# Where the multiplier table of the S5 scan is written: behind the initial states, at the end of a step

## The chip, the cores and the metric

The kernel runs on one core of a Trainium2 chip. The metric is the device time of one execution in microseconds (us), lower is better. The engines are named as in the profile: PE is TensorE (matmuls; PEld its weight loads), DVE is VectorE, ACT is ScalarE, POOL is GpSimd, and SP issues most of the DMAs. Each engine works through its own list of instructions in order, and waits on semaphores for the others.

## The reference, cut to what matters

A decoder of two layers works on 512 prompt tokens and on 8 x 4 sample tokens, 544 columns together. Layer 0 mixes tokens by gated linear attention, layer 1 by an S5 layer, and each is followed by an MLP of width 4096. The change lies in the S5 layer, a diagonal complex recurrence over the sequence:

```
u = xn @ w_in
bu = einsum(u, bb)                    # per group of 16 channels, 64 complex states
h[t] = lam * h[t-1] + bu[t]           # lam = mag * (cos + i sin), per state
y = Re(einsum(h, c)) + d_skip * u
z = gelu(y)
out = (z @ w_glu_a) * sigmoid(z @ w_glu_b)
```

All arithmetic is float32 in the result. Matmuls of the large weights are made of three products of high and low parts.

## The kernel before, in words

**Weights.** A large matrix is cut into tiles of 128 columns (1024 x 128). SP loads a tile `raw`; ACT casts it to the high part `wh` (L126, two halves of 128x512); DVE (L131) and POOL (L133) subtract to get the low part `wl`. A planner spreads these halves over the matmul jobs some jobs ahead of their use. One job is 24 matmuls on one tile and one half of the columns; a half is 288 or 256 columns.

**The recurrence.** The 64 groups of states are handled as 16 units. The complex recurrence is turned into a real one: every four tokens are gathered into one column (`n`), the values are rotated by a table of cosines and sines, a real scan with a decay per state runs along the 128 columns of prompt time, and the result is rotated back. The decay per step of four tokens is the column `self.r4`. The scan instruction wants a multiplier for each element, so `radius(u)` writes the table `rr` (128 x 2 x 2 x 128) with two ACT instructions at L1300 that copy a row of ones times `r4`. There is only one `rr`, so the table of unit u+1 may be written only after the scan of unit u has read it.

**Steps.** A software pipeline of steps (`beat(i)`), numbered -2 to 21, carries four units at once. In the order of the code, step i holds:

- `outs(i-3)`: PE multiplies the states by the output tables into `yp` (L1328, L1330); ACT makes the gelu (L1333); SP stores it to scratch `yd` (L1335).
- `states(i)`: PE makes the inputs of unit i, `wp` (L1273).
- `scan(i-2)`: DVE scans (L1308), then `radius(i-1)` on ACT (L1300), then, in some steps, `zl`, the low part of finished blocks of z (L1348), then the rotation back on DVE (L1312, L1313, L1314) and two tiny sums for the final state on POOL (L1317).
- `turned(i-1)`: POOL completes the rotation of unit i-1 (L1293, L1294), which its scan will read.
- `turn(i)`: DVE rotates `wp` of unit i (L1284, L1285, L1286); ACT copies the sample columns of `wp` into `S` (L1289, twice).
- loads by SP for later units: `load_q` (tables `qt` and `m`), `load_w` (`wt`, `ct`), `load_u` (`U`).
- `before(i-1)`: ACT writes the initial states of the samples into `area` (L1320).
- in some steps: ACT casts a finished block of z to `zh` (L1350), SP loads blocks of z (L1339).

`area` is one large buffer that holds the scan's input and output for two units, among other things; so the profile calls many of these tiles `area`.

The steps -2 to 11 are hung behind the jobs of the S5 input projection, one or two to a job:

```
BEATS = {5:(-2,),6:(-1,),7:(),8:(0,1),9:(2,),10:(3,4),11:(5,),12:(6,7),13:(8,),14:(9,10),15:(11,)}
```

So of the steps that scan, 2, 4, 5, 7, 8 and 10 are the last behind their job: the next things on ACT, DVE and POOL are the casts and subtractions of a weight tile (L126, L131, L133), then on DVE the evacuation of the job's PSUM bank (`u_out`, L1249), and only then the next scan. Steps 3, 6 and 9 are followed at once by another step, and so are 11 to 15, which run on after the last job with matmuls of the GLU that follows (`advance`, L237 on `zh`, `zl`) between them on PE.

Nothing is reordered: each engine gets its instructions in the order in which the code issues them.

Of the kernel before, what the change touches and what calls it, by code (L numbers as in the profile page):

```python
# [79 lines left out]
class Builder:  # L80
# [1105 lines left out]
    def s5(self, ctx):  # L1186
# [45 lines left out]
        def load_w(u):  # L1232
            for i in (0, 1):
                nc.sync.dma_start(table(u, i), self.wd[u][:, 512 * i:512 * i + 512])

        def load_q(u):
            if u < 16:
                nc.sync.dma_start(qt[u % NQ], self.qd[u])
                m = p.tile([128, 2, 128], F32, tag="m", name="m", bufs=NQ)
                for q in (0, 1):  # L1240
                    base = self.md[2 * u + q]
                    src = bass.AP(tensor=base.tensor, offset=base.offset, ap=[[256, 32], [32, 4], [1, 128]])
                    nc.sync.dma_start(m[:, q], src)
                st[u]["m"] = m
# [9 lines left out]
        def load_u(u):  # L1254
            if u < 16:
                m, q = divmod(u, 2)
                U = p.tile([128, 2, 136], F32, tag="U", name="U", bufs=6)
                d = self.ud[m]
                src = bass.AP(tensor=d.tensor, offset=d.offset + 272 * q, ap=[[4 * 136, 32], [128 * 136, 4], [1, 272]])
                nc.sync.dma_start(U.rearrange("p q n -> p (q n)"), src)  # L1260
                st[u]["U"] = U

        def cs(u):
            return table(u, 1).rearrange("p (t q n) -> p t q n", t=2, q=2)

        def states(u):

            w, U = table(u, 0), st[u]["U"]
            ps = []
            for r in (0, 1):  # L1270
                g = self.bank("wp")[:, :272].rearrange("p (q n) -> p q n", q=2)
                for q in (0, 1):
                    nc.tensor.matmul(g[:, q], w[:, r * 256 + q * 128:r * 256 + (q + 1) * 128], U[:, q],  # L1273
                                     start=True, stop=True)
                ps.append(g)
            st[u]["ps"] = ps

        def turn(u):

            ps, c = st[u].pop("ps"), cs(u)  # L1280
            tp = [self.p_t.tile([128, 288], F32, tag="sq", name="rot", bufs=5)[:, :256].rearrange("p (q n) -> p q n", q=2)
                  for _ in range(2)]
            re, im = ps[0][:, :, 8:136], ps[1][:, :, 8:136]
            V.tensor_mul(A["g"][u % 2], re[:, None].to_broadcast([128, 2, 2, 128]), c)  # L1284
            V.tensor_mul(tp[1], im, c[:, 1])  # L1285
            V.tensor_mul(tp[0], im, c[:, 0])  # L1286
            st[u]["tp"] = tp
            for r in (0, 1):
                nc.scalar.activation(ws[r][:, 2 * u:2 * u + 2], ps[r][:, :, 0:8], AF.Copy)  # L1289

        def turned(u):
            g, tp = A["g"][u % 2], st[u].pop("tp")
            G.tensor_tensor(g[:, 0], g[:, 0], tp[1], op=OP.add)  # L1293
            G.tensor_tensor(g[:, 1], tp[0], g[:, 1], op=OP.subtract)  # L1294

        def radius(u):

            ones = self.cst[:, C_ONE:C_ONE + 127]
            for q in (0, 1):
                nc.scalar.activation(rr[:, :, q, 1:128], ones[:, None].to_broadcast([128, 2, 127]), AF.Copy,  # L1300
                                     scale=self.r4[:, 2 * u + q:2 * u + q + 1])

        def scan(u, between):

            g, c = A["g"][u % 2], cs(u)
            oc, os = A["c"][u % 2][:, :, :, 9:137], A["s"][u % 2][:, :, :, 9:137]
            flat = lambda v: v.rearrange("p r q n -> p (r q n)")
            V.tensor_tensor_scan(flat(g), flat(rr), flat(g), 0.0, OP.mult, OP.add)  # L1308
            if u < 15:
                radius(u + 1)  # L1310
            between()
            V.tensor_mul(oc, g, c[:, None, 0].to_broadcast([128, 2, 2, 128]))  # L1312
            V.tensor_mul(os[:, 0], g[:, 0], c[:, 1])  # L1313
            V.scalar_tensor_tensor(os[:, 1], g[:, 1], -1.0, c[:, 1], op0=OP.mult, op1=OP.mult)  # L1314
            oc, os = A["c"][u % 2], A["s"][u % 2]
            for r in (0, 1):
                G.tensor_tensor(fs[:, r, 2 * u:2 * u + 2], oc[:, r, :, 136], os[:, 1 - r, :, 136], op=OP.add)  # L1317

        def before(u):
            nc.scalar.activation(A["c"][u % 2][:, :, :, 0:8], h0[:, :, 2 * u:2 * u + 2], AF.Copy)  # L1320

        def outs(u):
            s = st[u]
            q5 = qt[u % NQ]
            oc, os = A["c"][u % 2], A["s"][u % 2]
            ps = self.bank("yp")[:, :272].rearrange("p (q n) -> p q n", q=2)
            for q in (0, 1):
                nc.tensor.matmul(ps[:, q], s["m"][:, q], s["U"][:, q], start=True, stop=False)  # L1328
                for i, (r, h) in enumerate(((0, oc[:, 0]), (1, oc[:, 1]), (1, os[:, 0]), (0, os[:, 1]))):
                    nc.tensor.matmul(ps[:, q], q5[:, r * 256 + q * 128:r * 256 + q * 128 + 128], h[:, q, 0:136],  # L1330
                                     start=False, stop=(i == 3))
            y = A["y"][u % 2]
            nc.scalar.activation(y, ps, AF.Gelu_apprx_tanh)  # L1333
            m, half = divmod(u, 2)
            nc.sync.dma_start(self.yd[m].rearrange("t (e q) n -> (t e) q n", q=4)[:, 2 * half:2 * half + 2], y)  # L1335

        def load_z(m):
            for t in range(4):
                nc.sync.dma_start(A["z"][m % NZ][:, t], self.yd[m][3 - t])  # L1339

        def split_z(m, low):

            z = A["z"][m % NZ]
            if "h" not in Z:
                Z["h"] = self.p_p.tile([128, KD, NT], F32R, tag="Hh", name="zh")
            place = lambda v: v[:, m].rearrange("p (t c) -> p t c", t=4)
            if low:
                V.tensor_sub(place(Z["l"]), z, f32(place(Z["h"])))  # L1348
            else:
                nc.scalar.activation(place(Z["h"]), z, AF.Copy)  # L1350

        def beat(i):

            live = lambda j: 0 <= j < 16
            for m in Z_LOAD.get(i, ()):
                load_z(m)
            if live(i - 3):
                outs(i - 3)
            if live(i):
                states(i)  # L1360
            lo = lambda: [split_z(m, True) for m in Z_LOW.get(i, ())]
            if live(i - 2):
                scan(i - 2, lo)
            else:
                lo()
            if live(i - 1):
                turned(i - 1)
            if live(i):
                turn(i)
            if i >= 3:  # L1370
                load_q(i - 3 + NQ)
            if i in LW:
                load_w(LW[i])
            load_u(i + 2)
            if live(i - 1):
                before(i - 1)
            for m in Z_CAST.get(i, ()):
                split_z(m, False)
            for m in Z_LOAD_LAST.get(i, ()):
                load_z(m)  # L1380
# [10 lines left out]
        for s, beats in BEATS.items():  # L1391
            for i in beats:
                self.after[J + s].append(lambda i=i: beat(i))
# [5 lines left out]
        for i in range(done + 1, last + 1):  # L1399
            beat(i)  # L1400
            if i >= ZB + LAG:
                k = min((i - ZB - LAG) // 2 + 1, KD - 1)
                more = [(2, 0), (3, 0), (2, 1), (3, 1)][:max(0, i - FB + 1)]
                for t, hf in [(0, 0), (1, 0), (0, 1), (1, 1)] + more:
                    self.advance(self.tile0 + t, hf, zh, zl, k, t > 1)
# [206 lines left out]
```

## Time and profile before

| what | value |
|---|---|
| median of 3 runs (lowest, highest) | 1327.24 us (1324.19, 1329.14) |
| the profiled execution: its own time | 1327.25 us |
| the profiled execution: span of the trace | 1325.5 us |
| PE busy in the span | 1284.5 us (97%) |
| DVE busy | 746.7 us (56%) |
| ACT busy | 618.5 us (47%) |
| POOL busy | 445.9 us (34%) |
| first and last write of `rr` (L1300) | 722.4 us, 823.7 us |
| first and last scan (L1308) | 742.3 us, 827.0 us |
| in 738 to 842 us: PE, DVE, ACT, POOL busy | 93.05, 77.44, 39.32, 44.79 us of 104 |

How to read it: outside the S5 steps PE is busy all the time, and over the whole span it is busy 97%. The S5 steps lie between 738 and 842 us; there PE is idle for 11 us. In a timeline row the columns are start (us), duration of the merged pieces (us), engine, line, operation, output<-input, count, and in brackets the idle time of that engine just before the row with the instruction that is taken to have ended it. That name is inferred; where several semaphores were waited for, it need not be the one that decided.

### The profile page before, as it was taken

How to read it: one execution, taken by the hardware profiler on the slowest of the kernel's cores; microseconds unless marked ns; L12 is line 12 of the kernel's file. 1: busy time of each engine (PE TensorE's matmuls, PEld its weight loads, DVE VectorE, ACT ScalarE, POOL GpSimd, SP SyncE). 2: the span in 40 equal slices, each digit the busy share in tenths (PEclk: the TensorE clock that was granted, in tenths of full speed). 3: DMA queues.
4: the chain of work that ended last, by engine and by line, in shares of the span. 5: the costliest groups of instructions: out<-in, count | busy, mean ns of one | idle time of the engine just before them, and what ended most of it. 6: DMA issues, size and time to landing. Idle time of an engine off the chain costs nothing. (4 is left out here: it accounts for less than half of the span.)

```text
span 1325.5 us, 25660 instructions
## 1 busy us (share of the span) xinstructions
PE 1284.5 (97%) x9966; PEld 1260.1 (95%) x9966; DVE 746.7 (56%) x1747; ACT 618.5 (47%) x1394; POOL 445.9 (34%) x603
## 2 busy tenths in 40 slices
PE   7999999999999999999998988999999999999996
PEld 6999999999999999999998988999999999999996
DVE  7866564557436667666458678445721332332345
ACT  7633454566426657556444343446633432431432
POOL 4444244622371111111321443542223343242241
PEclk9999999999999999999999999999999999999998
DMA  5233322474324555545345688345523223232222
GB/s 192 96 132 107 104 69 84 129 183 99 105 81 162 156 165 175 169 139 154 100 119 182 185 249 239 98 138 135 121 65 112 80 80 96 80 96 80 80 65 68
DMA packets 83130, 164.67 MB, mean 124 GB/s; under 512 B 9313, under 2 KB 45409, under 8 KB 81985
## 3 DMA queue, kind: packets, MB, share of 16 engines
q1 hardware_dynamic: 77824, 144.16, 35.0%
q0 software_dynamic: 5184, 18.88, 6.3%
q8 instruction: 78, 1.28, 0.4%
q14 instruction: 44, 0.35, 0.1%
HBM read 137.54 MB, written 25.46 MB: 123 GB/s over the span
## 5 line engine op out<-in xcount | busy, mean ns | idle before, releaser
L133 POOL TENSOR_TENSOR wl<-raw,wh 128x384 fp32r<-128x384 f32 (+3 forms) x315 | 300.3, 964 | 549.0 <-ACT wh L126 544.0
L237 PE MATMUL held<-xh,wh 128*128 128x256 f32 (+1 forms) x1344 | 392.1, 292 | 0.1
L237 PE MATMUL held<-xl,wh 128*128 128x256 f32 (+1 forms) x1344 | 389.5, 290 | 0.0
L237 PE MATMUL held<-xh,wl 128*128 128x256 f32 (+1 forms) x1344 | 387.8, 289 | 0.1
L237 PE MATMUL held<-hh,wh 128*128 128x256 f32 (+1 forms) x1024 | 296.2, 289 | 0.7 <-ACT acc L440 0.7
L237 PE MATMUL held<-hl,wh 128*128 128x256 f32 (+1 forms) x1024 | 296.1, 289 | 0.0
L237 PE MATMUL held<-hh,wl 128*128 128x256 f32 (+1 forms) x1024 | 294.7, 288 | 0.0
L126 ACT ACTIVATE wh<-raw 128x512 fp32r<-128x512 f32 x332 | 198.6, 622 | 125.7 <-PE held L237 79.4
L237 PEld LDWEIGHTS held<-xh,wh 128*128 128x128 f32 x1344 | 254.4, 189 | 2.4 <-issue 1.4
L237 PEld LDWEIGHTS held<-xl,wh 128*128 128x128 f32 x1344 | 254.0, 189 | 0.4
L237 PEld LDWEIGHTS held<-xh,wl 128*128 128x128 f32 x1344 | 253.5, 189 | 0.3 <-DMA wl<-in_w 0.3
L131 DVE TENSOR_TENSOR wl<-raw,wh 128x128 fp32r<-128x128 f32 (+3 forms) x321 | 169.9, 542 | 106.8 <-ACT wh L126 100.4
L237 PEld LDWEIGHTS held<-hh,wh 128*128 128x128 f32 x1024 | 193.2, 189 | 2.6 <-issue 1.2
L237 PEld LDWEIGHTS held<-hl,wh 128*128 128x128 f32 x1024 | 193.0, 188 | 0.1
L237 PEld LDWEIGHTS held<-hh,wl 128*128 128x128 f32 x1024 | 192.6, 188 | 0.0
L432 ACT ACTIVATE r<-r 128x256 f32<-128x256 f32 (+1 forms) x128 | 55.0, 429 | 166.6 <-DVE r L430 166.5
L442 DVE TENSOR_TENSOR acc<-held,acc 128x288 f32<-128x288 f32 (+1 forms) x96 | 42.2, 439 | 120.8 <-PE held L237 120.7
L434 DVE TENSOR_TENSOR hl<-r,hh 128x256 fp32r<-128x256 f32 (+1 forms) x128 | 56.4, 441 | 83.1 <-ACT hh L433 82.6
L430 DVE SCALAR_TENSOR_TENSOR r<-held,rs 128x256 f32<-128x256 f32 (+1 forms) x128 | 56.1, 438 | 76.1 <-PE held L237 75.6
L237 PE MATMUL held<-zl,wh 128*128 128x288 f32 (+1 forms) x240 | 69.0, 288 | 1.4 <-DVE zl L1348 1.2
L237 PE MATMUL held<-zh,wh 128*128 128x288 f32 (+1 forms) x240 | 69.4, 289 | 0.0
L237 PE MATMUL held<-zh,wl 128*128 128x288 f32 (+1 forms) x240 | 68.7, 286 | 0.0
(393 smaller groups left out, 2044.3 us busy)
## 6 DMA issues: line engine op xcount, KB each, us to landing
raw<-in_w SPq DMA_DIRECT2D x166, 512.0 KB, 3.7
wh<-in_w POOLq DMA_DIRECT2D x18, 512.0 KB, 6.7
wl<-in_w POOLq DMA_DIRECT2D x18, 512.0 KB, 5.7
S<-in_h SPq DMA_DIRECT2D x4, 1024.0 KB, 5.0
out_gla_s<-S SPq DMA_DIRECT2D x4, 1024.0 KB, 3.8
wd<-blk SPq DMA_DIRECT2D x16, 256.0 KB, 2.9
wd<-cs SPq DMA_DIRECT2D x16, 256.0 KB, 3.3
qd<-blk SPq DMA_DIRECT2D x16, 256.0 KB, 2.8
```

Of the source, the lines that this page charges most:

```text
L126: nc.scalar.activation(h[:, a:c], r[:, a:c], AF.Copy)
L131: nc.vector.tensor_sub(l[:, a:b], r[:, a:b], f32(h[:, a:b]))
L133: nc.gpsimd.tensor_sub(l[:, b:c], r[:, b:c], f32(h[:, b:c]))
L237: self.nc.tensor.matmul(ps, a[:, k], cols(b, k), start=(k == 0 and i == 0), stop=(k == KD - 1 and i == 2))
L430: nc.vector.scalar_tensor_tensor(r[:, :n], ps, 0.0, self.rs[hf][:, :n], op0=OP.max, op1=OP.mult)
L432: nc.scalar.activation(r[:, :n], r[:, :n], AF.Square)
L434: self.late.append(lambda: nc.vector.tensor_sub(hl[:, m, c0:c1], r[:, :n], f32(h)))
L442: nc.vector.tensor_add(a, ps, a)
```

## The change

The call `radius(u + 1)` leaves `scan(u)`, where it stood right behind the scan instruction, and becomes `radius(i - 1)` in `beat(i)`, behind `before(i - 1)` and ahead of the casts of z. With u = i - 2 it is the same table in the same step, for the same steps 2 to 16 (`radius(0)` is written apart, in `open_area`). No instruction is added or removed.

```diff
@@ def scan(u, between):
             V.tensor_tensor_scan(flat(g), flat(rr), flat(g), 0.0, OP.mult, OP.add)
-            if u < 15:
-                radius(u + 1)
             between()
...
@@ def beat(i):
             load_u(i + 2)
             if live(i - 1):
                 before(i - 1)
+            if 2 <= i <= 16:
+                radius(i - 1)
             for m in Z_CAST.get(i, ()):
                 split_z(m, False)
```

Two lines fewer ahead of them give later lines of the function numbers that are smaller by two: L1312 to L1350 before are L1310 to L1348 after; L1300 and L1308 stay.

On ACT, steps 2 to 5 stand as follows before the change. In the rows, `rr` is the multiplier table (two instructions), `S_81` and `S_82` take the sample columns, `area<-h` are the initial states, `area<-yp` is the gelu and `wh<-raw` a weight cast. Step 3 begins behind the first weight cast shown, step 4 with the second gelu.

```order
L1300 ACTIVATE rr<-cst,r_3344 128x2x127 x2
L1289 ACTIVATE S_81<-wp 128x16
L1289 ACTIVATE S_82<-wp 128x16
L1320 ACTIVATE area<-h_8653 128x4x8
L126 ACTIVATE wh<-raw 128x512
L1333 ACT_TABLE_LOAD
L1333 ACTIVATE area<-yp 128x272
L1300 ACTIVATE rr<-cst,r_3344 128x2x127 x2
L1289 ACTIVATE S_81<-wp 128x16
L1289 ACTIVATE S_82<-wp 128x16
L1320 ACTIVATE area<-h_8653 128x4x8
L1333 ACTIVATE area<-yp 128x272
```

The same place on ACT after the change:

```order
L1289 ACTIVATE S_81<-wp 128x16
L1289 ACTIVATE S_82<-wp 128x16
L1318 ACTIVATE area<-h_8653 128x4x8
L1300 ACTIVATE rr<-cst,r_3344 128x2x127 x2
L126 ACTIVATE wh<-raw 128x512
L1331 ACT_TABLE_LOAD
L1331 ACTIVATE area<-yp 128x272
L1289 ACTIVATE S_81<-wp 128x16
L1289 ACTIVATE S_82<-wp 128x16
L1318 ACTIVATE area<-h_8653 128x4x8
L1300 ACTIVATE rr<-cst,r_3344 128x2x127 x2
L1331 ACTIVATE area<-yp 128x272
```

In each step `rr` has moved past the two copies into `S` and past the initial states, and now stands ahead of the weight cast (step 2) or of the next step's gelu (step 3).

On DVE the order is the same before and after. At this place (end of step 2, step 3, start of step 4), with the line numbers after the change:

```order
L131 TENSOR_TENSOR wl<-raw,wh 128x128
L1249 TENSOR_TENSOR us<-held,rs_85 128x72x4
L1308 SCALAR_TENSOR_TENSOR area<-rr,area 128x512
L1310 TENSOR_TENSOR area<-area,early 128x4x128
L1311 TENSOR_TENSOR area<-area,early 128x2x128
L1312 SCALAR_TENSOR_TENSOR area<-area,early 128x2x128
L1284 TENSOR_TENSOR area<-wp,early 128x512
L1285 TENSOR_TENSOR rot<-wp,early 128x256
L1286 TENSOR_TENSOR rot<-wp,early 128x256
L1308 SCALAR_TENSOR_TENSOR area<-rr,area 128x512
```

No row moved here; what moved is where `rr`, read by the last row, and `wh`, read by the first, stand on ACT relative to these rows.

## The prediction

> **What bounds the kernel now.** I read the page first: PE carries the run.
>
> ```profile
> PE 1284.5 (97%) x9966; PEld 1260.1 (95%) x9966; DVE 746.7 (56%) x1747; ACT 618.5 (47%) x1394; POOL 445.9 (34%) x603
> ```
>
> A change of order on ACT can only count where PE waits, so I read the S5 steps next: the sum over windows that cut 738 to 842 us (PE, PEld, DVE, ACT, POOL), and who waited for whom there, in the order PE, ACT, DVE (us in total, times, longest).
>
> ```profile
> sum 104.00, PE 93.05 PEld 90.54 DVE 77.44 ACT 39.32 POOL 44.79; mean PE 6.20 PEld 6.04 DVE 5.16 ACT 2.62 POOL 2.99
> ```
>
> ```profile
> PE yp L1330 <- ACT rr L1300: 4.3, 2, 2.9
> PE yp L1330 <- issue: 1.6, 1, 1.6
> ```
>
> ```profile
> ACT S L1289 <- DVE area L1284: 19.6, 15, 3.1
> ACT rr L1300 <- DVE area L1308: 12.8, 10, 2.8
> ```
>
> ```profile
> DVE wl L131 <- ACT wh L126: 11.2, 14, 1.5
> DVE zl L1348 <- ACT zh L1350: 8.3, 3, 4.3
> DVE area L1308 <- POOL area L1294: 4.5, 8, 1.8
> DVE area L1284 <- PE wp L1273: 1.1, 1, 1.1
> DVE us L1249 <- PE held L237: 0.7, 1, 0.7
> ```
>
> PE is idle 11 us of 104, and the largest entry names `rr`. That name is to be tested. Here is each of the two waits with DVE and ACT beside it; the last pair is the end of the recurrence (unit 15).
>
> ```profile
> 767.12 0.69 DVE L1312 TENSOR_TENSOR area<-area,early 128x512 f32<-128x512 f32 x1
> 767.18 0.91 ACT L1300 ACTIVATE rr<-cst,r 128x254 f32<-128x254 f32 x2 [1.41 <-DVE area L1308]
> ...
> 767.91 1.17 PE L1330 MATMUL yp<-area,qt 128*128 128x136 f32 x8 [1.42 <-ACT rr L1300]
> ...
> 786.25 0.69 DVE L1312 TENSOR_TENSOR area<-area,ct 128x512 f32<-128x512 f32 x1
> ...
> 787.04 2.15 PE L1330 MATMUL yp<-area,qt 128*128 128x136 f32 x8 [2.92 <-ACT rr L1300]
> ...
> 828.73 0.68 DVE L1312 TENSOR_TENSOR area<-area,ct 128x512 f32<-128x512 f32 x1
> ...
> 829.51 1.17 PE L1330 MATMUL yp<-area,qt 128*128 128x136 f32 x8 [1.62 <-issue]
> ```
>
> Each time PE starts 0.10 us after the end of L1312 (767.81, 786.94, 829.41): the rotated states, which these matmuls read. The `rr` pair of 767.18 ends at 768.09, after PE has started. So PE waits for DVE. And the list of DVE's waits has only two entries with PE in them, 1.1 and 0.7 us, once each, both ahead of the first scan (742.3 us):
>
> ```profile
> 738.53 0.69 DVE L1284 TENSOR_TENSOR area<-wp,early 128x512 f32<-128x512 f32 x1 [1.09 <-PE wp L1273]
> ...
> 741.84 0.59 DVE L1249 TENSOR_TENSOR us<-held,rs 128x256 f32<-128x256 f32 x1 [0.72 <-PE held L237]
> ```
>
> After that DVE never waits for PE; its pauses are weight casts, POOL and casts of z. So through the steps the chain is DVE's own list with the ACT work that it waits for, and PE trails it. What delays DVE there moves the start of the last output matmuls at 829.51. Behind that PE has no idle time that could take the delay up:
>
> ```profile
> 832.00:842.00 10.00, 10.00 (x78) 10.00 (x77) 3.04 (x4) 3.50 (x7) 5.77 (x8) 1.00 0.24 71
> ```
>
> **The change: what it may free.** Before, `rr` waits on ACT for the scan, with the copies into `S` behind it. But these copies wait for DVE in any case: the list has 15 times at which ACT stood idle in front of a copy until L1284 was done, 19.6 us, so `rr` was done before. The copies, the initial states, and the PSUM banks that the copies release come at the same time without `rr` ahead of them. Gain: nothing.
>
> **What it costs when another step follows at once (steps 3, 6, 9, 11 to 15).** Step 3 with the start of step 4:
>
> ```profile
> 751.93 0.42 DVE L1286 TENSOR_TENSOR rot<-wp,early 128x256 f32<-128x256 f32 x1
> 751.96 0.73 POOL L1294 TENSOR_TENSOR area<-rot,area 128x256 f32<-128x256 f32 x1
> 752.44 0.18 ACT L1289 ACTIVATE S<-wp 128x16 f32<-128x16 f32 x1 [0.54 <-DVE rot L1286]
> 752.52 0.22 ACT L1320 ACTIVATE area<-h 128x32 f32<-128x32 f32 x1
> 752.73 1.22 DVE L1308 TENSOR_TENSOR_SCAN area<-rr,area 128x512 f32<-128x512 f32 x1 [0.38 <-POOL area L1294]
> ```
>
> The second copy starts 0.09 us after L1286 (752.35). The scan of the next step waits for POOL until 752.69 and starts at 752.73, that is 0.38 us behind L1286. Now its multipliers are written only behind that copy and the initial states: `rr` starts 0.12 us after the start of the initial states (the spacing of ACT's rows in the next fence), 752.64, and ends 0.91 us later at 753.55; with 0.03 us to DVE the scan starts at 753.58 instead of 752.73: **+0.85 us**. Step 12 differs, as its scan does not wait for POOL:
>
> ```profile
> 805.75 0.42 DVE L1286 TENSOR_TENSOR rot<-wp,ct 128x256 f32<-128x256 f32 x1
> ...
> 806.21 1.23 DVE L1308 TENSOR_TENSOR_SCAN area<-rr,area 128x512 f32<-128x512 f32 x1
> ```
>
> 0.04 us becomes 1.23 us there, +1.19. Eight such steps: 7 x 0.85 + 1.19 = 7.1 us.
>
> **What it costs at the last step behind a job (2, 4, 5, 7, 8, 10).** Step 2:
>
> ```profile
> 745.91 0.42 DVE L1286 TENSOR_TENSOR rot<-wp,early 128x256 f32<-128x256 f32 x1
> ...
> 746.42 0.18 ACT L1289 ACTIVATE S<-wp 128x16 f32<-128x16 f32 x1 [0.54 <-DVE rot L1286]
> 746.50 0.22 ACT L1320 ACTIVATE area<-h 128x32 f32<-128x32 f32 x1
> 746.62 0.62 ACT L126 ACTIVATE wh<-raw 128x512 fp32r<-128x512 f32 x1
> ...
> 747.27 0.29 DVE L131 TENSOR_TENSOR wl<-raw,wh 128x128 fp32r<-128x128 f32 x1 [0.95 <-ACT wh L126]
> 747.48 0.65 DVE L1249 TENSOR_TENSOR us<-held,rs 128x288 f32<-128x288 f32 x1
> 747.98 1.53 DVE L1308 TENSOR_TENSOR_SCAN area<-rr,area 128x512 f32<-128x512 f32 x1
> ```
>
> `rr` itself is in time, but it now stands ahead of the weight cast. DVE has the subtraction L131 as its next instruction, waits for that cast, and holds L1249 and the scan behind it. A pair lasts 0.91 us with both halves overlapping their neighbours by about 0.09, so it takes 0.82 of ACT's list. Six steps x 0.82 = 4.9 us.
>
> Step 16 costs nothing: its scan waits much longer, for POOL.
>
> ```profile
> 826.97 1.22 DVE L1308 TENSOR_TENSOR_SCAN area<-rr,area 128x512 f32<-128x512 f32 x1 [1.82 <-POOL area L1294]
> ```
>
> **What takes some back.** In the steps where DVE waits for something that does not move with it, the delay fills that wait: 1.11 us for a cast of z that waits for its DMA, and 0.22 us in another.
>
> ```profile
> 801.74 0.73 DVE L1348 TENSOR_TENSOR zl<-area,zh 128x544 fp32r<-128x544 f32 x1 [0.22 <-DMA ud<-us]
> ...
> 813.69 0.73 DVE L1348 TENSOR_TENSOR zl<-z,zh 128x544 fp32r<-128x544 f32 x1 [1.11 <-ACT zh L1350]
> ```
>
> Also moved past: the gelus and with them SP's stores into `yd` come up to 0.8 us later against the step, and the loads `qt`, `m`, `wt`, `ct`, `U` queue behind them on SP. I cost this at nothing, because the DVE chain is later by more by then (at most 1 us more if the cover is gone). Casts of z behind `rr` have a scan of 1.2 us to hide in. PE's weights are cast several jobs ahead.
>
> **Sum.** 7.1 + 4.9 - 1.1 - 0.2 = 10.7 us later at 829.51, and so at the end. The profiled execution took 1327.25 us (span 1325.5), 0.01 us from the median of 1327.24: 1327.25 + 10.7 = **1338.0 us**.
>
> **PE's clock.** The longer waits of PE have a price of their own. The wait of 2.92 us is followed by a lower granted clock (the column ahead of the last two):
>
> ```profile
> 783.50:787.00 3.50, 0.62 (x4) 0.31 (x3) 3.46 (x5) 0.94 (x3) 1.64 (x2) 0.96 0.59 189
> 787.00:791.50 4.50, 4.46 (x25) 4.49 (x26) 3.92 (x8) 1.30 (x6) 1.72 (x4) 0.65 0.85 304
> ```
>
> 0.35 x 4.5 = 1.6 us of PE work lost. By the steps above DVE is later by 3.3 us at 767.12 (0.82 + 0.85 + 0.82 + 0.82, steps 2 to 5) and by 5.8 at 786.25 (0.85 + 0.82 + 0.82 more, steps 6 to 8). So the two waits grow to at most 1.42 + 3.3 = 4.7 and 2.92 + 5.8 - 3.3 = 5.4 us (PE itself is then 3.3 later). I cost the clock at nothing in the sum, since PE catches up in its next wait for DVE; the upper end takes 2 x 1.6 = 3.2 us. The Trainium skill, "TensorE: Matmul & The Clock Gate", the table of its Part 1, says that PE falls to half its clock after an idle window of about 3.4 us and needs as long of work to return. By that page each of the two waits would cost an estimated 1.7 us of PE work, 3.4 in all; the row at 787 shows such a drop already after 2.92 us.
>
> **The rivals.**
> 1. *Faster: PE or the ACT copies were held by `rr`.* If the named releaser is the true one, the 4.3 us vanish: 1327.25 - 4.3 = 1323.0. It decides if L1330 in fact starts with the end of an `rr` instruction. Against it: 0.10 us after L1312, three times, once with no `rr` near. 6%.
> 2. *No change: DVE has the room.* It is idle 26.6 us of 104; if a later scan were absorbed at each step (a spare of 0.85 us or more in front of the next one), 1327. Against it: the idle time consists of waits for ACT and POOL work that itself follows from DVE's step before. 8%.
> 3. *Only half of it.* If the weight casts at the ends of jobs do not hold DVE up (the scan there covered by PE's evacuation), 4.9 falls away: 10.7 - 4.9 = 5.8, 1333.0. Against it: L131 waited 14 times. 8%.
> 4. *The clock gate on top.* PE, slowed after both waits, becomes the later one again: 1338.0 + 3.2 = 1341.2. Against it: between the two waits DVE falls back by another 2.5 us (5.8 - 3.3), more than the 1.6 that PE loses, and after the second it falls back further. 9%.
>
> **How the numbers follow.** The forecast of 1338.0 has 69%. The range goes down to 1331.0 (rival 3 less 2 us, the spread of the runs before) and up to 1342.5 (12.0 us without anything taken back, plus 3.2 of clock, on 1327.25). About half a per cent, 6.6 us, is what a measurement of this kernel tells from no change, so slower begins at 1333.9: the forecast and rival 4 with a little of rival 3, 79%; within: rivals 2 and 3, 15%; faster 6%.
>
> **What would show it.** In the trace after: the scans of steps 4, 7, 10 and 12 to 16 wait for `rr`, not POOL, and start about 1.2 us behind L1286 (0.4 before); L131 of steps 2, 4, 5, 7, 8, 10 waits 0.8 us longer for its cast; PE's waits at L1330 grow to above 4 us twice; the last scan, before 84.7 us behind the first (742.3 to 827.0), comes 95 us behind it. The forecast is wrong if the scans keep their distance to L1286, or if PE's waits at L1330 shrink.

## The result, and the profile after

The changed kernel took 1337.46 us (median of 4 runs, 1336.84 to 1339.99), the kernel before 1325.72 us (median of 4, 1321.09 to 1329.14): a ratio of 1.0082, 95% interval 1.0063 to 1.0102 (the ratio on record; the two medians divided give 1.0089). Of the kernel before a fourth run was taken beside the changed one, so its median is 1.5 us below the one ahead of the prediction. The profiled execution took 1337.87 us with a span of 1336.1 us; before it was 1327.25 and 1325.5. The traces thus differ by 10.6 us, and what follows is read from them.

The engines do the same work in the same number of instructions (busy times of the page after):

```profile
PE 1287.3 (96%) x9966; PEld 1263.2 (95%) x9966; DVE 747.7 (56%) x1747; ACT 617.3 (46%) x1394; POOL 445.8 (33%) x603
```

The waits in the S5 steps have changed. First PE, then DVE, then ACT, after the change, over a window of 738 to 852 us that ends 10 us later than the 738 to 842 us before, as the steps do (us in total, times, longest; the lists in the prediction reach to 850 us, but the entries of them that are compared here all lie in the steps):

```profile
PE yp L1328 <- issue: 11.6, 5, 3.7
PE held L237 <- DVE zl L1346: 2.8, 2, 1.8
PE yp L1328 <- ACT rr L1300: 1.8, 1, 1.8
```

```profile
DVE wl L131 <- ACT wh L126: 12.6, 10, 2.3
DVE area L1308 <- ACT rr L1300: 10.6, 8, 1.6
DVE zl L1346 <- ACT zh L1348: 9.1, 2, 4.7
DVE area L1308 <- POOL area L1294: 1.8, 1, 1.8
```

```profile
ACT S L1289 <- DVE area L1284: 49.5, 15, 4.9
ACT rr L1300 <- DVE area L1308: 0.4, 1, 0.4
```

Eight scans (L1308) now wait for `rr`, 10.6 us in all; before, eight scans waited for POOL, 4.5 us, and of those one is left, that of the last unit. ACT itself no longer stops at `rr` (12.8 us before, 0.4 now) and stops at the copies into `S` for 49.5 us where it was 19.6: what it waited for at `rr` it now waits for at the copies (which grew by more than that), and nothing came earlier by it. PE waits longer, 11.6 us at the output matmuls.

Step 2 and the start of step 3 after the change, DVE and ACT (start, duration, engine, line, operation, tiles, and in brackets the idle time ahead and what ended it):

```profile
744.90 0.41 DVE L1286 TENSOR_TENSOR rot<-wp,early 128x256 f32<-128x256 f32 x1
...
745.41 0.18 ACT L1289 ACTIVATE S<-wp 128x16 f32<-128x16 f32 x1 [0.54 <-DVE rot L1286]
745.49 0.23 ACT L1318 ACTIVATE area<-h 128x32 f32<-128x32 f32 x1
745.61 0.89 ACT L1300 ACTIVATE rr<-cst,r 128x254 f32<-128x254 f32 x2
...
746.40 0.62 ACT L126 ACTIVATE wh<-raw 128x512 fp32r<-128x512 f32 x1
...
747.05 0.29 DVE L131 TENSOR_TENSOR wl<-raw,wh 128x128 fp32r<-128x128 f32 x1 [1.74 <-ACT wh L126]
```

The second copy and the initial states stand as close behind L1286 as before (0.10 us after its end, then 0.08). The cast `wh` starts 0.91 us behind the initial states where it was 0.12, and L131 waits 1.74 us instead of 0.95: 0.79 more. The end of step 3 with the start of step 4:

```profile
751.71 0.41 DVE L1286 TENSOR_TENSOR rot<-wp,early 128x256 f32<-128x256 f32 x1
...
752.22 0.18 ACT L1289 ACTIVATE S<-wp 128x16 f32<-128x16 f32 x1 [0.54 <-DVE rot L1286]
...
752.30 0.22 ACT L1318 ACTIVATE area<-h 128x32 f32<-128x32 f32 x1
752.42 0.89 ACT L1300 ACTIVATE rr<-cst,r 128x254 f32<-128x254 f32 x2
...
753.41 1.23 DVE L1308 TENSOR_TENSOR_SCAN area<-rr,area 128x512 f32<-128x512 f32 x1 [1.28 <-ACT rr L1300]
```

The scan starts 1.29 us behind the end of L1286 (752.12), 0.38 before: 0.91 more.

A clean measure of each step is the start of every scan, since the S5 steps are the same 16 in all kernels. The time from the first scan to the scan of each unit, in us, from the rows of L1308 (in the later kernels the line has another number):

| scan of unit | 1 | 2 | 3 | 4 | 6 | 8 | 9 | 11 | 12 | 13 | 14 | 15 |
|---|---|---|---|---|---|---|---|---|---|---|---|---|
| before | 5.69 | 10.44 | 16.17 | 23.27 | 34.77 | 47.15 | 53.18 | 63.92 | 68.45 | 75.23 | 79.75 | 84.68 |
| after | 6.48 | 12.14 | 18.62 | 26.49 | 39.62 | 53.69 | 60.14 | 72.68 | 78.03 | 84.52 | 89.87 | 94.80 |
| difference | 0.79 | 1.70 | 2.45 | 3.22 | 4.85 | 6.54 | 6.96 | 8.76 | 9.58 | 9.29 | 10.12 | 10.12 |

The delay grows at each step, and at the last scan it is 10.12 us. What follows that scan, after the change:

```profile
836.07 1.22 DVE L1308 TENSOR_TENSOR_SCAN area<-rr,area 128x512 f32<-128x512 f32 x1 [1.82 <-POOL area L1294]
...
838.62 2.15 PE L1328 MATMUL yp<-area,qt 128*128 128x136 f32 x8 [2.37 <-issue]
...
841.01 1.47 PE L1328 MATMUL yp<-area,qt 128*128 128x136 f32 x8
842.57 0.40 ACT L1331 ACTIVATE area<-yp 128x272 f32<-128x272 f32 x1 [6.12 <-PE yp L1328]
```

Before, the same two groups of matmuls lasted 1.17 and 1.09 us. From the last scan to the gelu it is 6.50 us (836.07 to 842.57); before it was 4.95 (826.97 to 831.92, the row below), so 1.55 us were lost there.

```profile
831.92 0.40 ACT L1333 ACTIVATE area<-yp 128x272 f32<-128x272 f32 x1 [4.08 <-PE yp L1330]
```

The granted clock (the column ahead of the last two) was 0.60 in the 4 us from the first of these matmuls on, after the change:

```profile
838.60:842.60 4.00, 3.98 (x21) 4.00 (x22) 0.58 (x2) 0.03 (x1) 3.10 (x7) 0.60 0.02 4
```

and 1.00 in the 2.4 us that the same work took before:

```profile
829.50:831.90 2.40, 2.39 (x20) 2.40 (x21) 0.58 (x2) 0.00 (x0) 1.66 (x5) 1.00 0.02 7
```

The bill of the two traces: 10.12 us in the steps, plus 1.55 us of slow matmuls at their end, less 1.02 us by which the first scan, which stands ahead of the first moved instruction, came earlier in this execution (741.27 against 742.29). That is 10.65 us, and the spans differ by 10.6. The last term is chance: in the profiled executions of all the kernels below, the first scan starts anywhere from 739.6 to 748.1 us.

### The profile page after: what moved, and what is told of

Its sections match the earlier page's. It is cut to its first block, busy times and chain, and to the rows that moved or that the text cites. A ratio compares the mean times of both kernels' runs of the same rounds, so it can differ in the third digit from the quotient of the medians.

```text
span 1336.1 us, 25647 instructions
## 1 busy us (share of the span) xinstructions
PE 1287.3 (96%) x9966; PEld 1263.2 (95%) x9966; DVE 747.7 (56%) x1747; ACT 617.3 (46%) x1394; POOL 445.8 (33%) x603
## 5 line engine op out<-in xcount | busy, mean ns | idle before, releaser
L133 POOL TENSOR_TENSOR wl<-raw,wh 128x384 fp32r<-128x384 f32 (+3 forms) x315 | 300.2, 964 | 555.0 <-ACT wh L126 550.0
L131 DVE TENSOR_TENSOR wl<-raw,wh 128x128 fp32r<-128x128 f32 (+3 forms) x321 | 171.3, 547 | 108.1 <-ACT wh L126 101.7
```

The costliest lines, as they stand in the source:

```text
L131: nc.vector.tensor_sub(l[:, a:b], r[:, a:b], f32(h[:, a:b]))
L133: nc.gpsimd.tensor_sub(l[:, b:c], r[:, b:c], f32(h[:, b:c]))
```

## The experiments

The theory to be tested is that of the prediction: the price is `rr` standing too late in two kinds of places (in front of a weight cast that DVE needs at once, and directly in front of the scan that reads it), each step adding its own share along DVE's list. Its rivals here: one of the two kinds is covered and the other carries all; or PE's longer waits, through the clock, carry a good part. And one question: does it matter that `rr` stands behind the copies at all, or only that it stands behind the last one?

**One part alone: the ends of jobs.** The kernel before, with `rr` late in steps 2, 4, 5, 7, 8 and 10 only.

```diff
+LATE_RR = (2, 4, 5, 7, 8, 10)
...
-            if u < 15:
+            if u < 15 and u + 2 not in LATE_RR:
                 radius(u + 1)
...
                 before(i - 1)
+            if i in LATE_RR:
+                radius(i - 1)
```

> The table is written late only in steps 2, 4, 5, 7, 8 and 10, the last ones behind a job; in the other steps it stays behind the scan as before. Theory of the chain (DVE's list with the ACT work it waits for sets the time): the weight cast starts 0.8 us later in these six steps, L131 and the scan with it; the last scan comes 4.2 us later against the first (the sum that the trace of the change shows for these steps), less up to 1.3 that fills DVE's waits for z: 3 to 4 us above before, 1.0022 to 1.0031 of it. Rival A (only a scan that has to wait for its own table costs): no change, because no scan waits for the table here. Rival B (the longer waits of PE cost through its clock, not through the list): nearly nothing, as PE's waits grow by 3 us at most.

Measured: 1331.02 us beside 1326.77, ratio 1.0031 (1.0017 to 1.0045). The last scan came 89.52 us behind the first, 4.84 later than before. That is more than the 4.2 us, less what DVE's waits for z fill, that were expected: in step 14 DVE waits 1.58 us for the cast of z where it waited 1.11, so this wait grew instead of filling up, and 0.48 of the 4.84 us come in there.

**The other part alone: steps followed at once.** The same edit with `LATE_RR = (3, 6, 9, 11, 12, 13, 14, 15, 16)`.

> The table is written late only in steps 3, 6, 9 and 11 to 16, behind which another step follows at once; in the steps that end a job it stays as before. Theory of the chain: eight scans start 0.8 to 0.9 us later behind L1286, 7.0 us in all, less 1.3 that fills DVE's waits for z: 5.7 us above before, up to 7.2 with a lower clock of PE at the end (1.0043 to 1.0054 of before). Rival A (only a scan that waits for its table costs): all of the change, 11 us, 1.008. Rival B (clock): nearly nothing.

Measured: 1331.28 us beside 1326.77, ratio 1.0042 (1.0026 to 1.0058). The last scan came 90.12 us behind the first, 5.44 later; the ratio is just below the range that was expected. In both parts alone the delay is there, so neither kind is covered. By scans they add up to 4.84 + 5.44 = 10.28 us, the whole change to 10.12; that they agree so closely is partly chance, as step 14 added to the first part and took 0.29 off the second and off the whole. The ratios add up to 1.0073; that the whole is larger, as its 1.55 us of slow matmuls would have it, lies within the intervals and isn't shown by them.

**How far behind.** `rr` between the two copies into `S`, instead of behind the copies and the initial states (in step 16, which has no copies, at the end).

```diff
             for r in (0, 1):
                 nc.scalar.activation(ws[r][:, 2 * u:2 * u + 2], ps[r][:, :, 0:8], AF.Copy)
+                if r == 0 and u >= 2:
+                    radius(u - 1)
...
             V.tensor_tensor_scan(flat(g), flat(rr), flat(g), 0.0, OP.mult, OP.add)
-            if u < 15:
-                radius(u + 1)
...
                 before(i - 1)
+            if i == 16:
+                radius(i - 1)
```

> The table is written between the two copies into S in each step, 0.5 us ahead of the end of L1286, behind the first copy alone. Theory of the chain: it is ready 0.44 us behind L1286, so a following scan loses 0.06 us and step 12 0.4; the weight casts lose 0.33 us in six steps: 0.8 + 2.0 = 2.8 us less up to 1.3: 1.5 to 2.8 above before, 1.001 to 1.002. Rival A (the place behind the step's waits costs as such): as the change, 11 us. Rival C (the scan alone must not wait): no change.

Measured: 1329.49 us beside 1326.77, ratio 1.0016 (1.0002 to 1.0030); the last scan 85.40 us behind the first, 0.72 later than before. The start of step 4 in it:

```profile
750.72 0.49 ACT L1302 ACTIVATE rr<-cst,r 128x254 f32<-128x254 f32 x1
751.12 0.17 ACT L1289 ACTIVATE S<-wp 128x16 f32<-128x16 f32 x1
...
751.32 1.22 DVE L1310 TENSOR_TENSOR_SCAN area<-rr,area 128x512 f32<-128x512 f32 x1 [0.45 <-ACT S L1289]
```

The second copy follows `rr` without a wait of its own, so `rr` has filled ACT's wait of 0.54 us for L1286, and the scan waits 0.45 us, about what it waited for POOL before. Ahead of the second copy `rr` costs 0.7 us over the steps, by the scans, instead of 10.1. That answers the question: ACT's idle time between the two copies is what `rr` can use, and behind the second copy there is none. The time lies in the range that was expected, but not by the sum behind it: L131 waits 1.09 us in step 2, 0.14 more than before, where 0.33 was expected for each weight cast. The median is 2.7 us above before, more than the 0.72 of the scans; the interval of the ratio, 0.3 to 4.0 us, holds both, and its profiled execution, 1326.34 us, does not show where the rest would be, so that stays open.

**Doubling the cost.** The changed kernel with `radius(i - 1)` called twice in each step; the second call writes the same values again.

```diff
             if 2 <= i <= 16:
                 radius(i - 1)
+                radius(i - 1)
```

> The changed kernel with the table written twice in a row at its new place. Theory of the chain: each of the 14 steps that pay does so for another 0.82 us: 11.5 us on top of the change, 1.016 to 1.019 of before; the scans of steps 4, 7, 10 and 12 to 16 start 2.05 us behind L1286. Rival A (the place costs, not the time that ACT needs there): as the change, 1.008. Rival B (ACT has room at job ends): only the eight followed steps pay, 6.6 us, 1.013.

Measured: 1348.86 us beside 1327.46, ratio 1.0156 (1.0133 to 1.0178). The last scan came 106.13 us behind the first, 11.33 later than after the change, whose own step was 10.12. The end of step 3:

```profile
753.08 0.41 DVE L1286 TENSOR_TENSOR rot<-wp,early 128x256 f32<-128x256 f32 x1
...
753.79 1.69 ACT L1300 ACTIVATE rr<-cst,r 128x254 f32<-128x254 f32 x4
...
755.58 1.23 DVE L1308 TENSOR_TENSOR_SCAN area<-rr,area 128x512 f32<-128x512 f32 x1 [2.08 <-ACT rr L1300]
```

Four instructions last 1.69 us where two last 0.89, 0.80 more; the scan starts 2.09 us behind the end of L1286 (753.49), 0.80 more than with one pair. The cost goes with ACT's time in front of the scan, as the theory has it (11.33 us by the scans, 11.5 expected; the ratio is just below the range that was expected). The rival by which the place alone costs had no further delay, and the one by which only the followed steps pay had 6.6 us.

**The clock at the end.** The changed kernel, with eight matmuls (16 in the trace's count) on data that are already there, ahead of the output matmuls of the last unit; their result is overwritten. PE then waits only briefly in front of the last output matmuls.

```diff
             ps = self.bank("yp")[:, :272].rearrange("p (q n) -> p q n", q=2)
+            for _ in range(8 if u == 15 else 0):
+                nc.tensor.matmul(ps[:, 0], s["m"][:, 0], s["U"][:, 0], start=True, stop=True)
```

> The changed kernel, with eight matmuls whose result is overwritten (1.9 us) ahead of the output matmuls of unit 15, so that PE is not idle for 2.4 us in its last wait for DVE. In the trace of the change these last matmuls ran slow (2.15 and 1.47 us for 8, against 1.17 and 1.09). Theory of the chain with the clock as a last term: they run at 1.17 and 1.09 again, and from the last scan to the end of these matmuls it takes 1.3 to 1.5 us less than after the change; the time is 0.1% below that of the change, which the times can hardly show. Rival (they were slow for another reason, a late table or a port): they stay at 2.15 and 1.47.

Measured: 1336.78 us beside 1327.46, ratio 1.0063 (1.0040 to 1.0085). The end of the steps in it:

```profile
839.65 2.02 PE L1326 MATMUL yp<-U,m 128*128 128x136 f32 x16
...
839.88 1.23 DVE L1308 TENSOR_TENSOR_SCAN area<-rr,area 128x512 f32<-128x512 f32 x1 [1.82 <-POOL area L1294]
...
842.42 1.17 PE L1330 MATMUL yp<-area,qt 128*128 128x136 f32 x8 [0.53 <-issue]
...
843.65 1.09 PE L1330 MATMUL yp<-area,qt 128*128 128x136 f32 x8
...
844.83 0.40 ACT L1333 ACTIVATE area<-yp 128x272 f32<-128x272 f32 x1 [4.59 <-PE yp L1330]
```

PE waits 0.53 us instead of 2.37, the granted clock is 1.00 (842.40 to 844.80 us), the two groups last 1.17 and 1.09 us again, and from the last scan to the gelu it is 4.95 us, as before the change. So the 1.55 us are the clock's, and come from PE's idle time there. The rival of PE's waits is right for this term alone. The trace shows it; the ratios (1.0063 and 1.0082) can't tell 1.55 us apart, and the profiled execution of this kernel, 1340.31 us, was the slowest of its five.

**The other way round: the casts first.** The kernel before, `rr` where it was, with the copies into `S` and the initial states behind the weight casts in the six steps that end a job. If ACT work in front of the cast costs what the theory says, taking away what stood there before should gain.

```diff
+JOB_ENDS = (2, 4, 5, 7, 8, 10)
...
             self.split_w(*u)
+        for f in self.behind_casts:
+            f()
+        self.behind_casts.clear()
...
-            for r in (0, 1):
-                nc.scalar.activation(ws[r][:, 2 * u:2 * u + 2], ps[r][:, :, 0:8], AF.Copy)
+            def copies():
+                for r in (0, 1):
+                    nc.scalar.activation(ws[r][:, 2 * u:2 * u + 2], ps[r][:, :, 0:8], AF.Copy)
+            self.behind_casts.append(copies) if u in JOB_ENDS else copies()
...
-                before(i - 1)
+                self.behind_casts.append(lambda: before(i - 1)) if i in JOB_ENDS else before(i - 1)
```

> The kernel before, but in steps 2, 4, 5, 7, 8 and 10 the copies into S and the initial states stand behind the next weight casts on ACT, not ahead of them; the table stays behind the scan. Theory of the chain: the cast is done when DVE comes to L131; DVE's waits there (0.95 in steps 2, 4, 5, 7; 1.2 and 1.5 in 10 and 8; 0.2 for each second cast) are gone, 7 us at most, of which PE can use what it waited for (L1330 5.9, zl 1.2): 4 to 7 us below before, 0.995 to 0.997. Rival B (PE's own list and clock set the time): no change. Rival D (copies moved back hold PSUM banks longer and PE waits for them): slower than before.

Measured: 1324.69 us beside 1326.77, ratio 0.9984 (0.9969 to 0.9999): faster, but by about 2 us only, half of the least that was expected. Up to unit 8 the scans gain 47.15 - 43.38 = 3.77 us, and at the last one 84.68 - 81.85 = 2.83 are left. L131 (here L133) no longer waits in step 2:

```profile
745.57 0.41 DVE L1291 TENSOR_TENSOR rot<-wp,early 128x256 f32<-128x256 f32 x1
745.90 0.61 DVE L133 TENSOR_TENSOR wl<-raw,wh 128x128 fp32r<-128x128 f32 x1
```

The gain is less than the wait: L133 lasts 0.61 us where L131 lasted 0.29, and of the 0.95 us the scan gains 0.52 (5.17 us behind the first instead of 5.69). Later, with DVE ahead, other waits come up or grow, for PE, for a z block, and on PE for `m` (3.8 us in two places, 1.4 before):

```profile
791.41 0.59 DVE L1254 TENSOR_TENSOR us<-held,rs 128x256 f32<-128x256 f32 x1 [1.41 <-PE held L242]
...
799.01 0.73 DVE L1356 TENSOR_TENSOR zl<-area,zh 128x544 fp32r<-128x544 f32 x1 [1.44 <-DMA yd<-area]
...
822.11 0.47 PE L1336 MATMUL yp<-U,m 128*128 128x136 f32 x2 [1.83 <-DMA m<-md]
```

**Both.** The same rearrangement on the changed kernel, `rr` too behind the weight casts at the ends of jobs.

> The changed kernel, but in steps 2, 4, 5, 7, 8 and 10 the copies into S, the initial states and the table stand behind the next weight casts on ACT. Theory of the chain: the cost at the job ends is gone (the table ends 1.2 us behind L1286, the scan comes there at 1.1 at the earliest) and the gain of casts first is had; the cost of the eight followed steps stays: 5.6 - 2.1 = 3.5 us above before at most, 1 at least: 1.001 to 1.0027. Rival A (a table at the end of a step costs as such): 1.008. Rival E (casts first hides all of it): not above before, 0.9985 to 1.

Measured: 1328.77 us beside 1327.46, ratio 1.0012 (0.9993 to 1.0031); the last scan 84.99 us behind the first, 0.31 later than before. Compared with the changed kernel the scans gain 9.81 us. DVE's waits in it:

```profile
DVE area L1316 <- ACT rr L1308: 11.0, 11, 1.3
```

Eleven scans wait for `rr` (eight after the change): the three more are behind steps 2, 4 and 10, and wait 0.19 to 0.24 us each. Behind the other three job ends no scan waits. The ratio lies in the range that was expected, but its interval also holds the rival by which nothing is left of the cost, and by the scans 0.31 us is left. Its profiled execution took 1334.99 us, 6 us above its median, and is used here for the scans alone.

**Loading ahead.** The casts-first kernel, with the loads of `qt` and `m` issued on SP ahead of the step's gelu store instead of behind it.

```diff
             nc.scalar.activation(y, ps, AF.Gelu_apprx_tanh)
+            if u >= 0:
+                load_q(u + NQ)
             m, half = divmod(u, 2)
...
-            if i >= 3:
-                load_q(i - 3 + NQ)
```

> The kernel before, with the copies of S and the initial states behind the weight casts at the job ends (as in the run of the casts first), and with the loads of qt and m issued on SP ahead of the step's gelu store instead of behind it. In the run of the casts first the last scan came 2.83 us earlier, and PE then waited 3.8 us for m in two steps. Theory: m is what holds the rest back, so without these waits the last scan and the end come 1 to 3 us earlier than there: 0.996 to 0.998 of the kernel before. Rival: the gelu stores stand behind the loads on SP, the transpose that brings z starts later by as much, and DVE and ACT wait for z instead: as the run of the casts first (0.998) or slower, with waits for z above the 1.44 us seen there.

Measured: 1323.91 us beside 1327.42, ratio 0.9972 (0.9957 to 0.9986), the best of the versions, though its interval overlaps that of the casts first. PE still waits for `m`, and SP now stops in front of the loads:

```profile
PE yp L1336 <- DMA m<-md: 3.3, 2, 1.9
```

```profile
SPq L1243 <- PE yp L1338: 4.4, 6, 1.4
```

The first row was 3.8 us there. `qt` and `m` have two buffers, and the load of the next waits until the output matmuls of this step have read theirs; passing the store saves little. The last scan came 81.92 us behind the first, no earlier than in the casts first (81.85). So the time lies in the range that was expected, but not for the reason given: the waits for `m` did not go, and the scans gained nothing. The rival was borne out in part: no wait for z is above the 1.44 us seen in the casts first, but a second one comes up, and they are 1.14 and 0.83 us. What made the time better, if it is better, isn't shown. Whether `m` is what holds the rest back would take a third buffer for it, and that wasn't tried.

## Why the prediction was right, and where not

*No gain from the move.* Right. ACT's wait moved from `rr` to the copies (12.8 to 0.4 us, 19.6 to 49.5), and the second copy stands 0.10 us behind L1286, as before.

*PE does not wait for `rr`.* Right. After the change the same matmuls are put down to "issue", and they still start 0.10 us behind the end of the DVE instruction that was L1312 and is now L1310:

```profile
769.32 0.69 DVE L1310 TENSOR_TENSOR area<-area,early 128x512 f32<-128x512 f32 x1
...
770.11 0.57 PE L1328 MATMUL yp<-area,qt 128*128 128x136 f32 x1 [3.47 <-issue]
...
790.87 0.69 DVE L1310 TENSOR_TENSOR area<-area,ct 128x512 f32<-128x512 f32 x1
...
791.66 0.56 PE L1328 MATMUL yp<-area,qt 128*128 128x136 f32 x1 [3.67 <-issue]
```

*Followed steps, +0.85 each, 7.1 in all.* From the scans: 0.91, 0.92, 0.89, 0.89 in steps 3, 6, 9 and 11, 0.91 in step 12, 0.82 and 0.83 in steps 13 and 15; in step 14 it is 0.29 less than nothing, the 0.85 with the wait for a cast of z taken off. The early steps were priced a little low. Step 12 was set at 1.19 with 0.22 taken back, 0.97 net, and that this is so near is in part luck. Its scan starts 1.64 us behind L1286 (813.95 against 812.31), not 1.23; `rr` has ended at 813.50, so what holds the scan for the last 0.35 us isn't shown. And a pause of DVE of 0.44 us in front of L1284, put down to "issue" before, is gone too; the prediction, which took DVE's pauses to be weight casts, POOL and casts of z, did not count it.

*Job ends, +0.82 each, 4.9 in all.* Steps 2, 4, 5, 7 and 8 cost 0.79, 0.75, 0.77, 0.71 and 0.80; step 10 cost 0.42. The term was mis-sized by 0.7 us (4.24 measured), 0.4 of it in step 10, which the prediction took to be like step 2 without reading its row. ACT was late there already before the change:

```profile
793.96 0.18 ACT L1289 ACTIVATE S<-wp 128x16 f32<-128x16 f32 x1 [0.83 <-DVE rot L1286]
...
794.82 0.29 DVE L131 TENSOR_TENSOR wl<-raw,wh 128x128 fp32r<-128x128 f32 x1 [1.24 <-ACT wh L126]
```

In step 2 the same copy started 0.09 us behind L1286; here it starts 0.38 behind its end (793.58). After the change this lateness is gone, and L131 waits as long as in step 2, 1.74 us:

```profile
800.77 0.29 DVE L131 TENSOR_TENSOR wl<-raw,wh 128x128 fp32r<-128x128 f32 x1 [1.74 <-ACT wh L126]
```

That is 0.50 more than before, where step 2 has 0.79 more. `rr` was not what made the copy late: it ended at 792.10, ahead of the first copy (792.95), and in the second part alone `rr` stands in front in step 10 as before, and the second copy starts 0.10 us behind the rotation (L1287 there, to 793.33):

```profile
790.53 0.91 ACT L1301 ACTIVATE rr<-cst,r 128x254 f32<-128x254 f32 x2
...
793.43 0.18 ACT L1290 ACTIVATE S<-wp 128x16 f32<-128x16 f32 x1 [0.54 <-DVE rot L1287]
```

What held the copy in the profiled execution before is not shown. So nothing here shows a gain of the move, and a part of its cost does not appear because the trace before was late in this step.

*Step 16 costs nothing.* Right: its scan waits 1.82 us for POOL in both traces.

*Taken back, 1.1 and 0.2.* The z cast that waited 1.11 us no longer waits after the change (in the first part alone this wait grew, so it does not stand still for every delay):

```profile
821.05 0.72 DVE L1346 TENSOR_TENSOR zl<-z,zh 128x544 fp32r<-128x544 f32 x1
```

*PE's clock, costed at nothing.* This step failed, at a place that the prediction did not look at. It asked only about the two waits in the middle of the steps. These grew to 3.47 and 3.67 us, not above 4 as it said: in front of the first, PE now waits 0.60 and 0.25 us in two earlier places (750.11 and 766.17) where it did not wait before. The granted clock was 0.62 behind the first (770.00 to 774.50 us), and behind the second 0.50:

```profile
791.60:796.50 4.90, 4.84 (x21) 4.87 (x22) 3.49 (x7) 1.65 (x6) 1.72 (x4) 0.50 0.77 270
```

There PE did catch up in later waits, as argued: the scans behind them grow by no more than the steps' own 0.8 to 0.9 us each. But the wait in front of the last output matmuls grew too, from 1.62 to 2.37 us, and behind it nothing waits for DVE any more, so its slow matmuls went into the end in full: 1.55 us, close to the 1.6 that the prediction put on one such event.

*The sum.* 10.7 us later at the last output matmuls was forecast. In the traces they start 9.11 us later (829.51 to 838.62), or 10.13 against the first scan, and the end of the steps comes 10.65 us later. The sum of the steps was 0.6 too high, the clock 1.55 too low, and the start of this execution 1.02 us early: the forecast of 1338.0 lies 0.5 us from the median of 1337.46 in part because these offset each other. Against the median of the four runs before, 1325.72, the change is 11.7 us, 1.0 more than forecast; these runs spread over 8 us, so that says little. The spread of the runs before that the range uses, 2 us, was also too small: the three lay between 1324.19 and 1329.14.

Of the rivals, the first (PE held by `rr`) and the second (DVE has the room) are refuted by the scans, the third by the two parts alone. (The 14 waits of L131 that were held against the third are counted up to 850 us; in the steps there are nine, at least one at each of the six job ends.) The fourth, the clock, came true in the size of one event, 1.55 us, but at a wait that it did not name; at the two that it named, PE caught up.

## What to carry to other kernels

A wait's named releaser is a hint: in this case the row that held PE was the one whose end lay 0.10 us ahead of the start in five places of two traces, and not the one that was named. Work of 0.9 us on an engine that is busy less than half of the time cost 0.7 to 0.9 us in most places behind that engine's wait, where what stands next was needed at once, and less than a tenth of it (0.72 us for 10.12, by the scans) in front of the wait. When a delay is followed to the end of a stage, look at the last wait on TensorE too: here the 1.55 us that the clock took there were not given back, and those in the middle were.

## What the hardware showed that was not expected

The granted clock of TensorE did not follow the length of the wait alone. After the change, matmuls ran slow behind a wait of 2.37 us (2.15 us for eight, where 1.17 is usual; granted clock 0.60); in the second part alone, a wait of 2.39 us at the same place in the program left them at full speed (granted clock 1.00 from 832.20 to 834.60 us):

```profile
832.23 1.17 PE L1331 MATMUL yp<-area,qt 128*128 128x136 f32 x8 [2.39 <-issue]
```

and in the kernel with both edits they were slow again behind 2.38 us (0.58 from 835.60 to 839.60 us):

```profile
835.66 2.15 PE L1336 MATMUL yp<-area,qt 128*128 128x136 f32 x8 [2.38 <-issue]
```

In the second part alone a wait of 3.13 us was followed by 1.87 us, between the two. The table in Part 1 of the Trainium skill's "TensorE: Matmul & The Clock Gate" has the clock fall after an idle window of about 3.4 us; the text below it says that this window runs freely. The traces agree that more than the wait's length decides, and differ in that the clock was lower behind waits of 2.37, 2.38 and 2.92 us, all shorter than that. What else decides, the place of the wait in such a window or the work just ahead of it, was not told apart.
